# The second mixer of a two-layer trunk: batched loads of B, K, keys, values and x, and stores issued by ScalarE

## The chip, the cores and the metric

The kernel runs on one core of a Trainium2 chip, as one program and in one launch. The metric is the device time of one execution in microseconds; the median of several executions is given. Five engines work side by side: PE (matmuls, with a separate row PEld for its weight loads), DVE and ACT (elementwise work and copies out of PSUM), POOL (small elementwise work and memsets) and SP, which here issues most of the DMAs. Each engine takes its instructions in a fixed order and waits on semaphores for the others.

## The reference

Two layers run over 1040 prompt tokens (16 learned ones ahead) and 64 tokens of a second group. Layer 0 mixes with a gated delta rule, layer 1 with RWKV-7; each is followed by a gated feed-forward part. The change touches the RWKV-7 mixer alone; in short form:

```python
xr, xw, xk, xv, xa, xg = h[None] + xx[None] * mu[:, None, None, :]
r, k, v = (xr @ w_r), (xk @ w_k), (xv @ w_v)
w_log = -softplus(-(w0 + tanh(xw @ w1) @ w2)) - 0.5
a = sigmoid(a0 + (xa @ a1) @ a2)
gate = sigmoid(xg @ g1) @ g2
kk = l2_normalize((k * k_k).reshape(B, T, RWKV_HEADS, RWKV_N))
k = k * (1.0 + (a - 1.0) * k_a)
decay = exp(-exp(w_log))
def step(S, inp):                      # per token, per head, S is 64 x 64
    d_t, kk_t, b_t, v_t, k_t, r_t = inp
    sa = einsum('bhij,bhj->bhi', S, -kk_t)
    S = S * d_t + sa[..., :, None] * b_t + v_t[..., :, None] * k_t
    return S, einsum('bhij,bhj->bhi', S, r_t)
y = group_norm(y) * ln_w + ln_b + sum(r * k * r_k) * v
x = x + (y * gate) @ w_o
```

## The kernel before

Everything is float32; a projection is done as three matmuls on a high and a low part of each operand (lines 130 to 132), with 1024 channels as eight tiles `f` of 128 and 1104 tokens as three groups `g`. The recurrence is computed by chunks of 64 tokens.

The mixer (`rwkv_a`, then `rwkv_b`) has these stages, and keeps what passes between them in DRAM tensors `dr[...]`, most of them eight tiles of 128 x 1152:

- Projection of r and the lora projections w, a and g. `store` writes r, the decay term SW and A (lines 1252 and 1265). The hidden part of the gate goes to HG.
- Key projection, `post_k`: per tile it loads A and SW, and stores PQ, KR[0], BK[0] and BK[1] (lines 1421 to 1428).
- Value projection, `post_v`: per tile it loads PQ, BK[1] and R (1455 to 1457), and stores KR[1], V and the bonus BV (1459 to 1467). The gram matrices of batch 0 and the first half batch are worked on beside it.
- The recurrence, six batches (three groups, four channel tiles each). In batch i, `weave` interleaves `chain` (the recurrence itself, two halves of three chunks), `build` for the half batches of batch i+1, `inverse` of batch i+1, `grams` of batch i+2 and `tail` of batch i-1 (norm, bonus, gate, and the output projection added to x). In batch 0 `gates` stands in the tail's place: it makes the gate from HG and stores it to GT (line 1169).

`build` loads for one channel tile of one half batch: bk by four transfers of 64 x 3 x 64 values (line 1553), kb by two of 64 x 2 x 192 (line 1555) and V by one (1556). The tiles kb live in one of three rooms `z` in turn, one of which lies in the freed space of xT; a room is written again when the chain has ended with the half batch three before. `tail` loads bonus and gate by two transfers (1747, 1749); then for each of eight output tiles it loads x, adds and stores it (1776, 1781, 1783). `inverse` solves 32 x 32 blocks on DVE and POOL, from the tile `dp`, whose last eight blocks are zero since the beginning.

The functions are generators; `weave` sets the order in which the program is written, and a scheduler then orders each engine's instructions by dependence and by its own reckoning, so the order on the engines can be seen only in the built program. Two rules of the program matter: an engine that issues a DMA first waits, in its order, until the data are written and the destination is free; and the DMAs of SP and ACT take one of eight semaphores in turn, and an issue waits until the last DMA on its semaphore has landed.

Of the kernel before, what the change touches and what calls it, by code (L numbers as in the profile page):

```python
# [9 lines left out]
F32 = mybir.dt.float32  # L10
F32R = mybir.dt.float32r
AF = mybir.ActivationFunctionType
ALU = mybir.AluOpType
# [3 lines left out]
P = 128  # L17
# [35 lines left out]
def tile_trunk(ctx, tc, *aps, stages=("gdn", "ffn0", "rwkv", "ffn1"), dbg=None):  # L53
    nc = tc.nc
# [6 lines left out]
    def uid(s):  # L61
        _n[0] += 1
        return f"{s}{_n[0]}"
# [71 lines left out]
    with ExitStack() as es:  # L135
# [6 lines left out]
        ps = psC()  # L142
# [1000 lines left out]
    def gates(tp, xp, dr):  # L1143
        w2 = ins["rwkv_g2"][0]
        hid = []
        for i in range(3):
            t = tp.tile([P, T], F32R, tag=f"hg{i}", bufs=1, name=uid("hg"))
            for c0, n in FULL:
                x = xp.tile([P, 384], F32, tag="ev", name=uid("hx"))
                nc.sync.dma_start(x[:, :n], dr["HG"][i, :, c0:c0 + n])  # L1150
                nc.scalar.copy(t[:, c0:c0 + n], x[:, :n])
            yield
            hid.append(t)
        raws = [rep2(w2[0:128], 1), rep2(w2[128:160], 4)]
        h, l, h2 = (tp.tile([P, KT, P], F32R, tag=f"g2{i}", bufs=1, name=uid("g2")) for i in range(3))
        split(h.rearrange("p a b -> p (a b)"), l.rearrange("p a b -> p (a b)"), raws[0])
        hf = h2.rearrange("p a b -> p (a b)")
        nc.scalar.copy(hf, raws[1])
        nc.vector.tensor_tensor(hf[64:128], raws[1][64:128], hf[64:128].bitcast(F32), ALU.subtract)
        terms = [(h, hid[0]), (h, hid[1]), (l, hid[0]), (h2, hid[2])]  # L1160
        yield
        for f in range(8):
            for g, (c0, n) in enumerate(LIVE):
                ps = psC()
                for i, (w, x) in enumerate(terms):
                    nc.tensor.matmul(ps[:, :n], w[:, f], x[:, c0:c0 + n], start=i == 0, stop=i == 3)
                o = tp.tile([P, 384], F32, tag="go", bufs=2, name=uid("go"))
                nc.scalar.copy(o[:, :n], ps[:, :n])
                nc.sync.dma_start(dr["GT"][f, :, (g + 1) * 384 - n:(g + 1) * 384], o[:, :n])
                yield  # L1170

    def hand_over(tp, xT, c0, n):
# [23 lines left out]
    def rwkv_a(hnp, col, prm, pc, plb, dr, esb, esx, esg, pend, esP):  # L1196
        C = math.exp(-0.5)
        with ExitStack() as es0, ExitStack() as es:
# [43 lines left out]
            def store(ps, n, g, f, name, func=AF.Copy, bias=0.0):  # L1242
                if name == "SW":
                    i = 2 if g else 1
                    e = (sv1 if g else sv0)[cnt[i] % 2]
                    cnt[i] += 1
                    if g == 0:
                        nc.scalar.activation(e[:, 0, 49:65], ps[:, 0:16], func, bias=bias)
                        nc.scalar.activation(e[:, 1:6, 1:65], ps[:, 16:n].rearrange("p (c t) -> p c t", t=64), func, bias=bias)
                    else:  # L1250
                        nc.scalar.activation(e[:, :, 1:65], ps[:, :n].rearrange("p (c t) -> p c t", t=64), func, bias=bias)
                    nc.sync.dma_start(dr["SW"][f, :, 6 * g:6 * g + 6], e)
                else:
                    if g == 0:
                        e = ev0[cnt[0] % 2]
                        cnt[0] += 1
                    else:
                        e = mp.tile([P, 384], F32, tag="ev", name=uid("ev"))
                    if func == AF.Copy and f % 2:
                        nc.vector.tensor_copy(e[:, 384 - n:], ps[:, :n])  # L1260
                    elif func == AF.Copy:
                        nc.scalar.copy(e[:, 384 - n:], ps[:, :n])
                    else:
                        nc.scalar.activation(e[:, 384 - n:], ps[:, :n], func, bias=bias)
                    nc.sync.dma_start(dr[name][f, :, g * 384:(g + 1) * 384], e)

            def dense(s, w, post):
                m = [None] * 3
# [128 lines left out]
            def post_k(ps, n, g, f):  # L1397
# [20 lines left out]
                nc.scalar.activation(c3(pq), l[:, :, 1:65], AF.Exp, scale=-C)  # L1418
                nc.gpsimd.tensor_copy(plb[:, f, 6 * g:6 * g + 6], c3(pq)[:, :, 63])
                cs = slice(g * 384, (g + 1) * 384)  # L1420
                nc.sync.dma_start(dr["PQ"][f, :, cs], pq)
                nc.vector.tensor_tensor(pe, kk, pe, ALU.mult)
                nc.sync.dma_start(dr["KR"][0, f, :, cs], pe)
                bh, kh = tmp("bh"), tmp("kh")
# [20 lines left out]
            with ExitStack() as es, ExitStack() as es1:  # L1445
# [5 lines left out]
                def post_v(ps, n, g, f):  # L1451
# [10 lines left out]
                    nc.tensor.matmul(pn[:, :384], bd1, kh, start=True, stop=True)  # L1462
                    e = ev0[f % 2] if g == 0 else mp.tile([P, 384], F32, tag="ev", name=uid("ev"))
                    nc.scalar.copy(e[:, o:], ps[:, :n])
                    nc.sync.dma_start(dr["V"][f, :, cs], e)
                    nc.vector.tensor_tensor(pq, pn[:, :384], e, ALU.mult)
                    nc.sync.dma_start(dr["BV"][f, :, cs], pq)

                d = dense(3, ins["rwkv_w_v"][0], post_v)
                for _ in range(4):  # L1470
# [24 lines left out]
    class batches:  # L1495
        def __init__(self, dr, tm):
# [5 lines left out]
                    nc.gpsimd.affine_select(mk[r, i], mk[r, i], pattern=[[1, 64]], compare_op=op, fill=0.0,  # L1502
                                            base=0, channel_multiplier=-1)
            self.mkb = mk.unsqueeze(1).to_broadcast([P, 3, 2, 64])
            self.dp = tm.tile([P, 32, 32], F32, tag="rdp", bufs=1, name="rdp")
            nc.gpsimd.memset(self.dp[:, 24:32], 0.0)
            self.pools, self.ttf = [], []

        def home(self, tp):
# [27 lines left out]
        def build(self, i, half):  # L1537
# [2 lines left out]
            tz = self.pools[min(z, 1)]  # L1540
            cs = slice(g * 384 + 192 * half, g * 384 + 192 * half + 192)
            W = B["W"][half] = tz.tile([P, 2, 3, 4, 64], F32, tag=f"W{z}", bufs=1, name=uid("W"))
            for ff in range(4):
                f = 4 * hf + ff
                kb = tz.tile([P, 2, 2, 192], F32, tag=f"kb{z}", bufs=4, name=uid("kb"))
                mb = tz.tile([P, 3, 64], F32, tag=f"mb{z}", bufs=4, name=uid("mb"))
                bt = tz.tile([P, 3, 128], F32, tag=f"bt{z}", bufs=4, name=uid("bt"))
                B["u"][half].append((kb, mb, bt))
                bk = tp.tile([P, 3, 2, 64], F32, tag="bk", bufs=3, name=uid("bk"))
                V = tp.tile([P, 192], F32, tag="V", bufs=2, name=uid("V"))  # L1550
                for q, r in enumerate(HR):
                    for a in range(2):
                        nc.sync.dma_start(bk[r, :, a ^ q], self.dr["BK"][a, f, r, cs].rearrange("p (c t) -> p c t", t=64))
                for q, r in enumerate(HR):
                    nc.sync.dma_start(kb[r, q], self.dr["KR"][:, f, r, cs].rearrange("a p c -> p a c"))
                nc.sync.dma_start(V, self.dr["V"][f, :, cs])
                pt = [psB(), psB()]
                pg = [p[:, :384].rearrange("p (c a t) -> p c a t", a=2, t=64) for p in pt]
                for j in range(3):
# [25 lines left out]
                yield  # L1585

        def inverse(self, i):
            B, tp, dp = self.at(i), self.tm, self.dp
            ttf, at = self.ttf[i % 2], B["at"]
            for b in range(4):  # L1590
                r = slice(32 * b, 32 * b + 32)
# [42 lines left out]
    def rwkv_b(xT, rc, col, plb, dr, Bx, gts, esx, esg, esf, esh, F, more):  # L1634
# [10 lines left out]
        with ExitStack() as esw, ExitStack() as es, ExitStack() as est:  # L1645
# [92 lines left out]
            def tail(g, hf, B):  # L1738
# [4 lines left out]
                cs = slice(g * 384 + o, (g + 1) * 384)  # L1743
                for ff in range(4):
                    f = 4 * hf + ff
                    bv = tp.tile([P, 384], F32, tag="lbv", bufs=lb, name=uid("lbv"))
                    nc.sync.dma_start(bv[:, :n], dr["BV"][f, :, cs])
                    gt = tp.tile([P, 384], F32, tag="lgt", bufs=lb, name=uid("lgt"))
                    nc.sync.dma_start(gt[:, :n], dr["GT"][f, :, cs])
                    pc_ = psC()  # L1750
                    m = 192 - o
                    for a, b, h in ((0, m, 0), (m, n, 1)):
# [8 lines left out]
                    nc.scalar.activation(rs, ps[:, :n], AF.Ln, bias=gne)  # L1761
                    nc.scalar.activation(rs, rs, AF.Exp, scale=-0.5)
                    nc.vector.scalar_tensor_tensor(rs, pc_[:, :n], col("rwkv_ln_w", f), rs, ALU.mult, ALU.mult)
                    nc.vector.scalar_tensor_tensor(rs, rs, col("rwkv_ln_b", f), bv[:, :n], ALU.add, ALU.add)
                    nc.vector.tensor_tensor(rs, rs, gt[:, :n], ALU.mult)
                    split(yy[0][:, ff, :n], yy[1][:, ff, :n], rs)
                    yield
                c0 = LIVE[g][0]
                for mp in range(4):
                    u = wunit(w_o[512 * hf:512 * hf + 512, 256 * mp:256 * mp + 256].rearrange("(k p) c -> p k c", p=P), *wpo)  # L1770
                    wv = [t.rearrange("p (k m) c -> p k m c", m=2) for t in u]
                    for mm in range(2):
                        m = 2 * mp + mm
                        if g < 2:
                            xt = tp.tile([P, 384], F32, tag="xt", bufs=4, name=uid("xt"))[:, :n]
                            nc.sync.dma_start(xt, dr["X"][:, m, c0:c0 + n])
                        else:
                            xt = xT[:, m, c0:c0 + n]
                        ps = psC()
                        mm3(ps[:, :n], (wv[0][:, :, mm], wv[1][:, :, mm]), yy, range(4), n)  # L1780
                        nc.vector.tensor_tensor(xt, xt, ps[:, :n], ALU.add)
                        if g < 2:
                            nc.sync.dma_start(dr["X"][:, m, c0:c0 + n], xt)
                        yield

            def first(tp, hp):
                F.silu = True
# [166 lines left out]
    if dbg and "x" in dbg:  # L1954
        nc.sync.dma_start(dbg["x"], xT)
    if "rwkv" in stages:
        rs_ = {k: dp_.tile([8, P, 1152], F32, name="r" + k) for k in ("V", "GT", "BV", "R")}
        for k in ("KR", "BK"):
            rs_[k] = dp_.tile([2, 8, P, 1152], F32, name="r" + k)
        rs_["X"] = dx  # L1960
        more = "ffn1" in stages
        F, esf, esh = rwkv(xfull, dx, rs_, rc, col, prm, pc, more, pend, esP)
# [46 lines left out]
```

## Time and profile before

| | us |
|---|---|
| median of three timed runs | 3351.06 (3349.12 to 3355.72) |
| the profiled execution's own time | 3353.38 |
| its span, first to last instruction | 3351.6 |
| key projection, value projection (from the trace) | 1770 to 1905, 1905 to 2066 |
| batches 0 to 3 of the recurrence | 2066 to 2160, to 2240, to 2318, to 2398 |

The span is that of one profiled execution; some 2 us lie around it. In the rows below, `xT` also stands for rooms that are cut out of the freed space of the tile xT. A row of waits reads "engine line waited for: total, times, longest"; a row of the chain "start, length, what"; a row of one line's instructions gives the smallest, median and largest duration in ns. SPq and ACTq are the queues of SP and ACT that issue DMAs.

### The profile page before, as it was taken

The page shows a single profiled execution, that of the slowest core. Times are in us where ns is not written, and L with a number is a line of the kernel's source. Part 1 is how long each engine was busy: PE and PEld are TensorE (multiplying, and loading weights), DVE is VectorE, ACT ScalarE, POOL GpSimd, SP SyncE. Part 2 cuts the span into 40 slices and gives each one's busy share as a digit, 9 for nine tenths or more (in the row PEclk, how much of TensorE's full clock was granted, in tenths as well). Part 3 has the DMA queues.
Part 4 walks back from the last instruction along what each step waited for, and adds up shares of the span by engine and source line. Part 5 has one row for each costly group of instructions (what it writes and reads, how often), then busy time and mean ns, then how long its engine had stood idle before and what let it go on. Part 6 is the DMA issues. An engine that isn't in the chain of part 4 may idle for free. (4 is left out here: it accounts for less than half of the span.)

```text
span 3351.6 us, 69660 instructions
## 1 busy us (share of the span) xinstructions
PE 3177.9 (95%) x27426; PEld 2983.6 (89%) x27426; DVE 2505.8 (75%) x5011; ACT 1561.5 (47%) x3134; POOL 293.1 (9%) x539
## 2 busy tenths in 40 slices
PE   7999999898999999999999888888999999999998
PEld 6888888798999999999998777677778999999998
DVE  6967867467777667766879874889986687877775
ACT  5866766434433333213778733434455443333112
POOL 1000000002200000000001130533300310000000
PEclk9999999999999999999999999989999999999999
DMA  5433332884332225422256876445565333335231
GB/s 167 118 99 101 105 91 71 293 278 138 97 98 82 78 75 169 131 83 88 76 184 194 279 227 211 134 141 164 161 192 170 105 97 97 94 94 175 85 98 61
DMA packets 543912, 452.49 MB, mean 135 GB/s; under 512 B 78377, under 2 KB 494930, under 8 KB 543458
## 3 DMA queue, kind: packets, MB, share of 16 engines
q1 hardware_dynamic: 538682, 445.61, 43.2%
q8 instruction: 216, 3.54, 0.4%
q10 hardware_dynamic: 4904, 2.43, 0.3%
q14 instruction: 110, 0.90, 0.1%
HBM read 306.86 MB, written 141.07 MB: 134 GB/s over the span
## 5 line engine op out<-in xcount | busy, mean ns | idle before, releaser
L311 PE MATMUL psA<-tc,sh 128*128 128x276 f32 (+1 forms) x1712 | 500.2, 292 | 20.4 <-DVE hs L319 9.4
L313 PE MATMUL psA<-tc,sl 128*128 128x276 f32 (+1 forms) x1712 | 499.9, 292 | 4.0 <-DVE sl L110 3.9
L312 PE MATMUL psA<-tc,sh 128*128 128x276 f32 (+1 forms) x1712 | 499.4, 292 | 0.3 <-DVE tc L110 0.2
L407 DVE TENSOR_TENSOR xT<-xT,psA 128x384 f32<-128x384 f32 (+3 forms) x496 | 252.4, 521 | 135.0 <-PE psA L132 133.2
L311 PEld LDWEIGHTS psA<-tc,sh 128*128 128x128 f32 x1712 | 327.0, 191 | 22.6 <-DVE hs L319 10.1
L109 ACT CAST wh<-raw 128x1024 fp32r<-128x1024 f32 x159 | 166.3, 1049 | 357.8 <-PE psA L131 239.9
L313 PEld LDWEIGHTS psA<-tc,sl 128*128 128x128 f32 x1712 | 326.5, 191 | 5.0 <-DVE sl L110 4.7
L312 PEld LDWEIGHTS psA<-tc,sh 128*128 128x128 f32 x1712 | 326.6, 191 | 1.2 <-DVE tc L110 0.9
L131 PE MATMUL psA<-hl,wh 128*128 128x384 f32 (+3 forms) x1024 | 326.4, 319 | 0.0
L130 PE MATMUL psA<-hh,wh 128*128 128x384 f32 (+3 forms) x1024 | 325.7, 320 | 0.0
L132 PE MATMUL psA<-hh,wl 128*128 128x384 f32 (+3 forms) x1024 | 325.3, 318 | 0.0
L130 PE MATMUL psA<-hnh,wh 128*128 128x384 f32 (+1 forms) x768 | 269.9, 351 | 5.4 <-ACT hnh L109 4.1
L131 PE MATMUL psA<-hnl,wh 128*128 128x384 f32 (+1 forms) x768 | 262.3, 341 | 1.7 <-DVE hnl L110 1.7
L132 PE MATMUL psA<-hnh,wl 128*128 128x384 f32 (+1 forms) x768 | 261.0, 340 | 0.0
L110 DVE TENSOR_TENSOR wl<-raw,wh 128x1024 fp32r<-128x1024 f32 x159 | 195.0, 1228 | 66.0 <-ACT wh L109 65.5
L109 ACT CAST sh<-raw 128x512 fp32r<-128x512 f32 x202 | 124.9, 621 | 254.9 <-PE psA L312 235.0
L130 PE MATMUL psA<-mxh,wh 128*128 128x384 f32 (+1 forms) x672 | 225.0, 345 | 10.6 <-ACT mxh L109 5.6
L131 PE MATMUL psA<-mxl,wh 128*128 128x384 f32 (+1 forms) x672 | 229.7, 344 | 1.9 <-DVE mxl L110 1.6
L132 PE MATMUL psA<-mxh,wl 128*128 128x384 f32 (+1 forms) x672 | 226.8, 339 | 0.3 <-DVE wl L110 0.3
L130 PEld LDWEIGHTS psA<-hh,wh 128*128 128x128 f32 x1024 | 192.0, 188 | 0.6 <-ACT hh L109 0.4
L132 PEld LDWEIGHTS psA<-hh,wl 128*128 128x128 f32 x1024 | 192.4, 188 | 0.1
L131 PEld LDWEIGHTS psA<-hl,wh 128*128 128x128 f32 x1024 | 192.2, 188 | 0.3
(490 smaller groups left out, 8204.3 us busy)
## 6 DMA issues: line engine op xcount, KB each, us to landing
raw<-in_ffn_w_gate_dram SPq DMA_DIRECT2D x64, 512.0 KB
raw<-in_ffn_w_up_dram SPq DMA_DIRECT2D x64, 512.0 KB
raw<-in_ffn_w_down_dram SPq DMA_DIRECT2D x44, 512.0 KB
raw<-in_gdn_w_in_dram SPq DMA_DIRECT2D x32, 512.0 KB
raw<-in_gdn_w_out_dram SPq DMA_DIRECT2D x24, 512.0 KB
raw<-in_rwkv_w_o_dram SPq DMA_DIRECT2D x24, 512.0 KB
hr<-dhid SPq DMA_DIRECT2D x44, 276.0 KB
hr<-dhid SPq DMA_DIRECT2D x44, 272.0 KB
```

The lines of the kernel that those rows point to most:

```text
L109: nc.scalar.copy(h, src)
L110: (eng or nc.vector).tensor_tensor(l, src, h.bitcast(F32), ALU.subtract)
L130: nc.tensor.matmul(ps, w[0][:, k, :], x[0][:, k, :n], start=a, stop=False)
L131: nc.tensor.matmul(ps, w[0][:, k, :], x[1][:, k, :n], start=False, stop=False)
L132: nc.tensor.matmul(ps, w[1][:, k, :], x[0][:, k, :n], start=False, stop=z)
L311: nc.tensor.matmul(ps, u[0][:, kk], h, start=first and kk == 0, stop=False)
L312: nc.tensor.matmul(ps, u[0][:, kk], l, start=False, stop=False)
L313: nc.tensor.matmul(ps, u[1][:, kk], h, start=False, stop=last and kk == 3)
L407: nc.vector.tensor_tensor(xT[:, m, a:a + n], xT[:, m, a:a + n], pd[:, :n], ALU.add)
```

## The change

- V, PQ, R (even tiles), A, SW and the gate are stored by ACT's queue, which wrote them, instead of SP's.
- BV and GT become one tensor BG, and `tail` loads both parts with one transfer.
- `build` loads kb for all four channel tiles of a half batch at its start, by four transfers of 64 x 4 x 192; bk and V for two channel tiles at a time.
- `tail` loads and stores x by two output tiles, and issues a store only after the first addition of the next pair.
- `dp` is no longer kept: it shares the buffer `b32b` with a later tile of the inverse, and POOL clears its last blocks each time.

```diff
-                nc.sync.dma_start(dr["GT"][f, :, (g + 1) * 384 - n:(g + 1) * 384], o[:, :n])
+                nc.scalar.dma_start(dr["BG"][1, f, :, (g + 1) * 384 - n:(g + 1) * 384], o[:, :n])
...
-                    nc.sync.dma_start(dr["SW"][f, :, 6 * g:6 * g + 6], e)
+                    nc.scalar.dma_start(dr["SW"][f, :, 6 * g:6 * g + 6], e)
...
-                    if func == AF.Copy and f % 2:
+                    q = nc.sync if func == AF.Copy and f % 2 else nc.scalar
+                    if q is nc.sync:
...
-                    nc.sync.dma_start(dr[name][f, :, g * 384:(g + 1) * 384], e)
+                    q.dma_start(dr[name][f, :, g * 384:(g + 1) * 384], e)
...
-                nc.sync.dma_start(dr["PQ"][f, :, cs], pq)
+                nc.scalar.dma_start(dr["PQ"][f, :, cs], pq)
...
-                    nc.sync.dma_start(dr["V"][f, :, cs], e)
+                    nc.scalar.dma_start(dr["V"][f, :, cs], e)
                     nc.vector.tensor_tensor(pq, pn[:, :384], e, ALU.mult)
-                    nc.sync.dma_start(dr["BV"][f, :, cs], pq)
+                    nc.sync.dma_start(dr["BG"][0, f, :, cs], pq)
...
+            f0 = 4 * hf
+            kbs = tz.tile([P, 4, 2, 2, 192], F32, tag=f"kb{z}", bufs=1, name=uid("kb"))
+            for q, r in enumerate(HR):
+                for a in range(2):
+                    nc.sync.dma_start(kbs[r, :, q, a], self.dr["KR"][a, f0:f0 + 4, r, cs].rearrange("f p c -> p f c"))
             for ff in range(4):
-                f = 4 * hf + ff
-                kb = tz.tile([P, 2, 2, 192], F32, tag=f"kb{z}", bufs=4, name=uid("kb"))
+                if ff % 2 == 0:
+                    fs = slice(f0 + ff, f0 + ff + 2)
+                    bks = tp.tile([P, 2, 2, 192], F32, tag="bk", bufs=2, name=uid("bk"))
+                    for q, r in enumerate(HR):
+                        for a in range(2):
+                            nc.sync.dma_start(bks[r, :, a ^ q], self.dr["BK"][a, fs, r, cs].rearrange("f p c -> p f c"))
+                    Vs = tp.tile([P, 2, 192], F32, tag="V", bufs=2, name=uid("V"))
+                    nc.sync.dma_start(Vs, self.dr["V"][fs, :, cs].rearrange("f p c -> p f c"))
+                kb, V = kbs[:, ff], Vs[:, ff % 2]
+                bk = bks[:, ff % 2].rearrange("p a (c t) -> p c a t", t=64)
...
-                bk = tp.tile([P, 3, 2, 64], F32, tag="bk", bufs=3, name=uid("bk"))
-                V = tp.tile([P, 192], F32, tag="V", bufs=2, name=uid("V"))
-                for q, r in enumerate(HR):
-                    for a in range(2):
-                        nc.sync.dma_start(bk[r, :, a ^ q], self.dr["BK"][a, f, r, cs].rearrange("p (c t) -> p c t", t=64))
-                for q, r in enumerate(HR):
-                    nc.sync.dma_start(kb[r, q], self.dr["KR"][:, f, r, cs].rearrange("a p c -> p a c"))
-                nc.sync.dma_start(V, self.dr["V"][f, :, cs])
...
-            B, tp, dp = self.at(i), self.tm, self.dp
+            B, tp = self.at(i), self.tm
+            dp = tp.tile([P, 32, 32], F32, tag="b32b", bufs=1, name=uid("rdp"))
+            nc.gpsimd.memset(dp[:, 24:32], 0.0)
...
-                    bv = tp.tile([P, 384], F32, tag="lbv", bufs=lb, name=uid("lbv"))
-                    nc.sync.dma_start(bv[:, :n], dr["BV"][f, :, cs])
-                    gt = tp.tile([P, 384], F32, tag="lgt", bufs=lb, name=uid("lgt"))
-                    nc.sync.dma_start(gt[:, :n], dr["GT"][f, :, cs])
+                    bg = tp.tile([P, 2, 384], F32, tag="lbg", bufs=lb, name=uid("lbg"))
+                    nc.sync.dma_start(bg[:, :, :n], dr["BG"][:, f, :, cs].rearrange("a p c -> p a c"))
...
+                    if g < 2:
+                        xt = tp.tile([P, 2, 384], F32, tag="xt", bufs=2, name=uid("xt"))[:, :, :n]
+                        nc.sync.dma_start(xt, dr["X"][:, xs, c0:c0 + n])
...
                     for mm in range(2):
...
-                        nc.vector.tensor_tensor(xt, xt, ps[:, :n], ALU.add)
-                        if g < 2:
-                            nc.sync.dma_start(dr["X"][:, m, c0:c0 + n], xt)
+                        nc.vector.tensor_tensor(xt[:, mm], xt[:, mm], ps[:, :n], ALU.add)
+                        if late:
+                            nc.sync.dma_start(*late)
+                            late = None
                         yield
+                    if g < 2:
+                        late = dr["X"][:, xs, c0:c0 + n], xt
+                if late:
+                    yield
+                    nc.sync.dma_start(*late)
```

The scheduler orders the engines anew. On SP, in the middle of the value projection, before (rV, rKR and rBV are stores, pq, kh and rt loads of one tile each, raw a weight):

```order
L1465 DMA rV<-ev_17768 128x384
L1455 DMA pq_22214<-rPQ 128x384
L1467 DMA rBV<-pq_22147 128x384
L1456 DMA kh_22345<-rBK 128x384
L1457 DMA rt_22346<-rR 128x384
L1556 DMA V_22560<-rV 128x192
L117 DMA raw_22586<-in_rwkv_w_v_dram 128x8x128
L1459 DMA rKR<-rt_22216 128x384
L1465 DMA rV<-ev_22225 128x384
L1467 DMA rBV<-pq_22214 128x384
```

and now, at a like place:

```order
L1460 DMA rKR<-rt_21990 128x384
L1458 DMA rt_22061<-rR 128x384
L117 DMA raw_22578<-in_rwkv_w_v_dram 128x8x128
L1456 DMA pq_22059<-rPQ 128x384
L1457 DMA kh_22147<-rBK 128x384
L1468 DMA rBG<-pq_21988 128x384
L1458 DMA rt_22148<-rR 128x384
```

The stores of V are gone from SP; the other two stores of a tile stay among its loads.

On ACT, in the key projection, before (pe, pi and pq are three exponentials of one tile, sq of the next ones):

```order
L1416 ACTIVATE pe_20410<-sw_20395 128x384
L1417 ACTIVATE pi_20411<-sw_20395 128x384
L1418 ACTIVATE pq_20412<-sw_20395 128x384
L1407 ACTIVATE sq_20519<-sq_20519 128x336
L1403 ACTIVATE sq_20575<-psA_20546,prm 128x384
```

and now:

```order
L1417 ACTIVATE pe_20293<-sw_20278 128x384
L1418 ACTIVATE pi_20294<-sw_20278 128x384
L1419 ACTIVATE pq_20295<-sw_20278 128x384
L1404 ACTIVATE sq_20338<-psA_20309,prm 128x384
L1422 DMA rPQ<-pq_20295 128x384
L1404 ACTIVATE sq_20396<-psA_20367,prm 128x384
```

The store of pq stands on ACT, one activation behind the one that writes it. Of the 132 moved stores 98 stand so, with at least one instruction between; 34 follow their write directly.

On SP, in batch 2, where the keys for the second half of batch 3 are loaded (raw is a weight of the output projection), before:

```order
L117 DMA raw_26682<-in_rwkv_w_o_dram 128x4x256
L1776 DMA xt_26688<-dx 128x320
L1553 DMA bk_26709<-rBK 64x3x64 x4
L1555 DMA kb_26706<-rKR 64x2x192 x2
L1556 DMA V_26710<-rV 128x192
L1776 DMA xt_26772<-dx 128x320
L117 DMA raw_26849<-in_rwkv_w_o_dram 128x4x256
L1776 DMA xt_26855<-dx 128x320
L1553 DMA bk_26888<-rBK 64x3x64 x4
L1555 DMA kb_26885<-rKR 64x2x192 x2
```

and now, for the same half batch:

```order
L1553 DMA bk_26549<-rBK 64x2x192 x4
L1555 DMA V_26554<-rV 128x2x192
L1526 DMA b_26838<-rBK 128x384
L1753 DMA lbg_26359<-rBG 128x2x320
L1527 DMA k_26839<-rKR 128x384
L1546 DMA kb_26544<-rKR 64x4x192 x4
L1753 DMA lbg_27225<-rBG 128x2x384
L1553 DMA bk_26891<-rBK 64x2x192 x4
L1555 DMA V_26896<-rV 128x2x192
```

The keys of all four tiles are asked for by four transfers in a row, and what followed the first two of eight now follows all of them.

More of the change, by code (lines that the diff above doesn't have):

```diff
@@ L1504, in __init__ @@
             self.mkb = mk.unsqueeze(1).to_broadcast([P, 3, 2, 64])
-            self.dp = tm.tile([P, 32, 32], F32, tag="rdp", bufs=1, name="rdp")
-            nc.gpsimd.memset(self.dp[:, 24:32], 0.0)
             self.pools, self.ttf = [], []
@@ L1763, in tail @@
                     nc.vector.scalar_tensor_tensor(rs, pc_[:, :n], col("rwkv_ln_w", f), rs, ALU.mult, ALU.mult)
-                    nc.vector.scalar_tensor_tensor(rs, rs, col("rwkv_ln_b", f), bv[:, :n], ALU.add, ALU.add)
-                    nc.vector.tensor_tensor(rs, rs, gt[:, :n], ALU.mult)
+                    nc.vector.scalar_tensor_tensor(rs, rs, col("rwkv_ln_b", f), bg[:, 0, :n], ALU.add, ALU.add)
+                    nc.vector.tensor_tensor(rs, rs, bg[:, 1, :n], ALU.mult)
                     split(yy[0][:, ff, :n], yy[1][:, ff, :n], rs)
@@ L1771, in tail @@
                     wv = [t.rearrange("p (k m) c -> p k m c", m=2) for t in u]
-                    for mm in range(2):
-                        m = 2 * mp + mm
-                        if g < 2:
[L1775 to L1778, printed above, removed]
+                    xs = slice(2 * mp, 2 * mp + 2)
+                    if g < 2:
+                        xt = tp.tile([P, 2, 384], F32, tag="xt", bufs=2, name=uid("xt"))[:, :, :n]
+                        nc.sync.dma_start(xt, dr["X"][:, xs, c0:c0 + n])
+                    else:
+                        xt = xT[:, xs, c0:c0 + n]
+                    for mm in range(2):
                         ps = psC()
                         mm3(ps[:, :n], (wv[0][:, :, mm], wv[1][:, :, mm]), yy, range(4), n)
-                        nc.vector.tensor_tensor(xt, xt, ps[:, :n], ALU.add)
-                        if g < 2:
-                            nc.sync.dma_start(dr["X"][:, m, c0:c0 + n], xt)
+                        nc.vector.tensor_tensor(xt[:, mm], xt[:, mm], ps[:, :n], ALU.add)
+                        if late:
+                            nc.sync.dma_start(*late)
+                            late = None
                         yield
+                    if g < 2:
[3 more added lines that the diff above has]
+                    nc.sync.dma_start(*late)
             def first(tp, hp):
@@ L1956, in tile_trunk @@
     if "rwkv" in stages:
-        rs_ = {k: dp_.tile([8, P, 1152], F32, name="r" + k) for k in ("V", "GT", "BV", "R")}
-        for k in ("KR", "BK"):
+        rs_ = {k: dp_.tile([8, P, 1152], F32, name="r" + k) for k in ("V", "R")}
+        for k in ("KR", "BK", "BG"):
             rs_[k] = dp_.tile([2, 8, P, 1152], F32, name="r" + k)
```

## Prediction

> **What bounds the kernel now.** I read the page first, then a table of stages, then the waits of each stage, then the chain that ended last.
>
> ```profile
> span 3351.6 us, 69660 instructions
> PE 3177.9 (95%) x27426; PEld 2983.6 (89%) x27426; DVE 2505.8 (75%) x5011; ACT 1561.5 (47%) x3134; POOL 293.1 (9%) x539
> ```
>
> PE is busy 95% of the span, so what an edit can give back is in the stages where PE is not busy. The change touches the second mixer alone. The view of stages (start:end, length, then busy time of PE, PEld, DVE, ACT and POOL, granted clock, DMA share, GB/s) shows, in order: the lora projections, the key projection, the value projection, batch 0 with the gates, and batches 2 and 3 of the recurrence. The last line is a short piece of batch 1.
>
> ```profile
> 1657.00:1712.00 55.00, 49.39 (x274) 46.40 (x273) 45.78 (x96) 46.30 (x102) 2.84 (x8) 0.97 0.51 153
> 1770.00:1905.00 135.00, 122.50 (x636) 109.27 (x635) 123.83 (x228) 112.66 (x233) 22.12 (x39) 0.96 0.75 243
> 1905.00:2066.00 161.00, 144.78 (x1141) 124.73 (x1141) 105.01 (x212) 60.41 (x122) 30.31 (x63) 0.95 0.77 238
> 2066.00:2160.00 94.00, 81.78 (x1536) 67.65 (x1535) 70.92 (x168) 41.09 (x97) 31.71 (x71) 0.90 0.47 132
> 2240.00:2318.00 78.00, 69.47 (x1285) 57.93 (x1286) 72.23 (x168) 35.11 (x78) 27.41 (x58) 0.96 0.57 163
> 2318.00:2398.00 80.00, 70.78 (x1259) 58.82 (x1256) 73.41 (x166) 35.42 (x78) 25.53 (x55) 0.94 0.58 166
> 2197.00:2206.00 9.00, 9.00 (x155) 7.14 (x154) 7.84 (x21) 4.27 (x11) 0.00 (x0) 1.00 0.18 48
> ```
>
> PE idles 12.5 us in the key projection, 16.2 in the value projection, 12.2 in batch 0 and 8 to 9 in a later batch, where DVE is busy 72 of 78 us and its work is untouched. Which of this idle time ends with a DMA? Waits of engines, first in the value projection, then (last line) in the key projection; columns are total, times, longest:
>
> ```profile
> PE psC L1462 <- DVE kh L1460: 10.5, 8, 2.3
> DVE rt L1458 <- DMA pq<-rPQ: 13.8, 7, 5.1
> ACT hg L1151 <- DMA hx<-rHG: 14.8, 8, 4.6
> ACT wh L109 <- DMA raw<-in_rwkv_w_v_dram: 4.0, 2, 2.2
> ```
>
> And the waits of the queue that issues, SP: the first line over the whole run, the others from 1950 to 2570 us.
>
> ```profile
> SPq L1421 <- ACT pq L1418: 29.8, 18, 9.1
> SPq L1783 <- DVE xt L1781: 28.6, 12, 7.6
> SPq L1783 <- DVE b32t L601: 12.4, 9, 3.9
> SPq L1465 <- ACT ev L1464: 7.4, 8, 1.5
> SPq L1455 <- DMA rBV<-pq: 4.8, 9, 1.1
> ```
>
> So SP does stand still behind stores, with loads queued behind it. But the place where it stands longest costs nothing:
>
> ```profile
> 2195.15 2.54 SPq L1553 DMA_DIRECT2D bk<-rBK  x4
> 2205.35 0.33 SPq L1783 DMA_DIRECT2D dx<-xt  x1
> 2205.72 1.42 SPq L1555 DMA_DIRECT2D kb<-rKR  x2
> ```
>
> From 2197.7 to 2205.3 SP waits to store x, and a key load waits behind it; in that piece PE is busy 9.00 of 9.00 us (last row of the stages). Removed SP waits therefore count only where a stage shows that somebody was late. The chain that ended last names four loads in the recurrence:
>
> ```profile
> 2078.31 3.25 DMA k<-rKR
> ...
> 2150.75 3.47 DMA xT<-rKR
> ...
> 2311.86 3.13 DMA lgt<-rGT
> ...
> 2364.99 2.45 DMA xT<-rKR
> ```
>
> (xT<-rKR is a key load into the room of xT.)
>
> **The change part by part.** The profiled execution took 3353.4 us, 2.3 over the median of the three timed runs; the terms go against it. What an issue costs:
>
> ```profile
> L1421 SPq DMA_DIRECT2D rPQ<-pq x24: 319/320/571, 1768.5 to 1893.0; - x24
> L1553 SPq DMA_DIRECT2D bk<-rBK x192: 573/605/1717, 1919.2 to 2451.3; - x192
> L1555 SPq DMA_DIRECT2D kb<-rKR x64: 573/607/1596, 2063.4 to 2438.8; - x64
> L1169 SPq DMA_DIRECT2D rGT<-go x24: 319/537/1442, 2060.9 to 2155.4; - x24
> L901 ACTq DMA_DIRECT2D dSZ<-sz x6: 366/370/397, 558.6 to 602.7; - x6
> ```
>
> *Issues that go from SP.* 192 loads of bk become 96 and 96 of kb (64 and 32 into xT) become 48: 96 x 0.605 + 48 x 0.607 = 87 us of SP. 132 stores go to ACT, about 132 x 0.32 = 42 us, more for the gates. SP is not the bound, so I price stage by stage what is late.
>
> *Into the value projection.* ACT waits 4.0 us for two weight loads there. On SP the loads stand behind stores of pq, which wait for ACT. Most of the wait is the transfer itself; I take 1 us saved, from 0 to 4.
>
> *Value projection.* PE waits 10.5 us for kh, which is late because DVE waits 13.8 us for pq loads. The stores of V leave SP (7.4 us of its waits), the wait of a pq load for the landing of the store from the same buffer (4.8) stays, and so does the round trip. I take a third of PE's 10.5, 3.5 us, from 0 to 10.5. The hx loads hold ACT for 14.8 us at the end, while PE still has projections to do; 1 us, from 0 to 5.
>
> *Batch 0.* 24 x 0.537 = 12.9 us of gate stores and about a third of the load issues go from SP; the chain has one 3.25 us load of k, and PE idles 12.2 us of which DVE and ACT end most. 3 us, from 0 to 8.
>
> *Later batches.* The x stores now come one step later (a tail's last one two), and half as many, so SP no longer waits 28.6 + 12.4 us for them; by the piece from 2197 this was covered. One merged load of bonus and gate saves an issue ahead of the 3.13 us lgt load: 1 us, from 0 to 7.
>
> *The key loads get larger.* A half batch now starts with four loads of 192 KB where its first tile needed two of 96 KB. The room comes free only when an earlier half batch has ended, about when the build begins, so they can't be early. Before: 2 x 0.607 plus 2.45 to 3.47 to land, 3.7 to 4.7 us. After: 4 x 0.607 plus the 3.25 us that a 192 KB load of k took, 5.7 us. That is 1 to 2 us more for the first tile, and less for the next three. Two of eleven half batches had such a load in the chain: 2 us lost, from 0 to 11 x 2 = 22. I stay near the low end because only those two show.
>
> *Stores on ACT.* A row of before shows what an issue there costs:
>
> ```profile
> 558.59 0.53 ACT L225 ACTIVATE sg<-sg 128x384 f32<-128x384 f32 x1
> 558.65 0.40 ACTq L901 DMA_DIRECT2D dSZ<-sz  x1
> 559.15 0.53 ACT L226 ACTIVATE sg<-sg 128x384 f32<-128x384 f32 x1
> ```
>
> The queue issues while the engine still computes, and the next activation starts on time. In the built order an activation stands between write and store in most cases, so the cost is near 0; 34 stores (14 of V, 16 of the gates, 4 of R) follow their own write, 34 x 0.37 = 12.6 us, nearly all in stages where ACT is busy 60.41 of 161 and 41.09 of 94 us. If the cover is gone, the key projection pays: ACT 112.66 + 24 x 0.37 = 121.5 of 135. The lora stage, with the 24 stores of SW, would go from 46.30 to 55.2 of 55 if nothing overlapped. I take 1 us lost, from 0 to 13. A new wait comes with it: DMAs share eight semaphores in turn, so an ACT store may wait until an older DMA of SP has landed, and the PSUM copies queue behind it. Three PSUM buffers, each filled by one of 24 tiles in 161 us (about 6.7 us a tile), cover a landing of 3 us.
>
> *The pad of the inverse* moves into a shared buffer and is set in each of six inversions by POOL, which is busy 27.41 of 78 us. The nearest row sets four times as much:
>
> ```profile
> L1598 POOL MEMSET b32t<- x6: 952/952/1099, 1901.7 to 2380.1; 128x1024 f32 x6
> ```
>
> 0, from 0 to 6 x 0.95 = 5.7 lost. The bk matmuls read the same runs of 64 values: 0. The granted clock (0.90 to 0.96 in these stages) I leave as it is.
>
> Sum: -1 -3.5 -1 -3 -1 +2 +1 = -6.5 us, so 3346.9 for the profiled execution; taken from the median 3351.06 it is 3344.6, rounded to **3345**.
>
> **The Trainium skill against it.** The Trainium skill, DMA: Bandwidth & Descriptors, section "Issuing engines are not separate DMA queues", says that transfers begun on several engines run on the same 16 DMA engines, and that only the sequencer's time to begin them is saved. By that rule the moved stores give the 42 us of SP's issue time and nothing else; the piece from 2197 agrees, and it speaks for the second rival. The Trainium skill, Perfetto Trace Analysis, section "DMA Optimizations", says that where DMA engines are mostly idle, splitting a transfer lets some of the work start sooner. The recurrence has a DMA share of 0.47 to 0.58, so that rule speaks against the large key loads, and for the third rival.
>
> **Rivals.**
> 1. *The DMA round trips were the bound of the value projection and batch 0.* For it: the 13.8 and 14.8 us of waits. Against: the round trip remains. It would give all of the upper ends there, 4 + 10.5 + 5, and 2.5 in batch 0, less 2 of loss: -20, 3331.
> 2. *It is hidden anyway.* SP waited, but nobody for SP. For it: PE full during the longest stall, DVE busy 72 of 78 us per batch. Time 3351.
> 3. *The first key tile comes late.* Place: the first tile of a half batch, whose room is freed at a batch's start or in its middle. Each of 11 half batches pays 1 to 2 us, and PE's fixed order puts the recurrence behind it: 11 x 1.5 = +16, less 4 of gains, 3363. It decides from the point where a first tile's matmuls stand within 5.7 us behind the last matmul that read the old keys. Against: PE has the other half's work to do.
>
> **How the numbers follow.** Chances: small gain (3337 to 3351) 0.55, rival 1 0.15, rival 2 0.10, rival 3 0.20. A measurement of this kernel can tell 0.2%, 6.7 us, from no change, so the line is at 3344.4: half of the small gain and rival 1 make 0.42 faster; the other half, rival 2 and a little of rival 3 make 0.39 same; 0.19 slower. The likeliest case alone spans 3337 to 3351. The range for 8 in 10 takes half of rival 1 and most of rival 3: 3328 to 3364.
>
> **What would show it.** Right: the value projection shorter by 3 to 6 us with fewer waits of DVE for pq; batches 2 and 3 within 2 us of 78 and 80; ACT's store rows near 0.37 us with no new idle time behind them. Wrong: key loads in the chain at the start or middle of batches with waits over 5 us (rival 3); ACT idle before its PSUM copies with a DMA named; or the value projection shorter by over 12 us (rival 1). A changed order on PE that moves a stage by several us without a DMA wait would be outside of this reckoning.

## The result, and the profile after

The changed kernel takes 3375.26 us (median of 6 runs), the kernel before 3349.11 in the runs beside it: a ratio of 1.0076, with a 95% interval of 1.0061 to 1.0092. The prediction was 3345 us, and its range ended at 3364. The head of the page of the changed kernel:

```profile
span 3373.9 us, 69301 instructions
...
PE 3179.6 (94%) x27426; PEld 2984.5 (88%) x27426; DVE 2496.9 (74%) x5011; ACT 1563.0 (46%) x3134; POOL 299.9 (9%) x544
```

The engines do the same work, and the span is 22.3 us longer, so time went into waiting or into a slower clock. To find where, I cut both traces at the same instructions and not at the same times. The view of stages of the kernel before, from the first SW sigmoid to the first exponential of the key projection (called the **lora stretch** below), then to the first copy of the value projection, to its last copy, to the start of batch 1's chain, and to the end of batch 5 (columns as above: length, busy time of PE, PEld, DVE, ACT, POOL, granted clock, DMA share, GB/s):

```profile
1664.41:1767.60 103.19, 98.13 (x550) 92.65 (x550) 74.06 (x151) 75.92 (x166) 6.49 (x22) 0.98 0.52 167
1767.60:1913.08 145.48, 132.00 (x684) 118.00 (x685) 133.63 (x247) 119.43 (x247) 22.51 (x40) 0.95 0.76 245
1913.08:2059.41 146.33, 131.97 (x1085) 113.11 (x1083) 94.43 (x189) 52.34 (x105) 30.31 (x63) 0.97 0.77 235
2059.41:2159.69 100.28, 86.20 (x1546) 71.42 (x1546) 73.27 (x176) 43.66 (x103) 31.40 (x71) 0.88 0.49 140
2159.69:2545.18 385.49, 349.99 (x5754) 292.16 (x5754) 329.13 (x739) 173.61 (x377) 103.23 (x211) 0.94 0.54 159
```

The same five stretches of the changed kernel:

```profile
1659.79:1785.46 125.67, 106.51 (x550) 99.22 (x550) 75.06 (x152) 81.90 (x169) 6.82 (x22) 0.91 0.43 138
1785.46:1934.24 148.78, 131.93 (x678) 119.59 (x679) 132.38 (x244) 118.68 (x247) 16.36 (x40) 0.93 0.74 237
1934.24:2087.80 153.56, 134.05 (x1092) 116.28 (x1090) 95.84 (x191) 52.86 (x108) 31.36 (x64) 0.96 0.77 238
2087.80:2180.19 92.39, 80.49 (x1567) 66.19 (x1568) 68.85 (x166) 43.86 (x104) 27.87 (x57) 0.96 0.59 177
2180.19:2566.27 386.08, 347.77 (x5736) 288.12 (x5732) 324.59 (x749) 172.79 (x377) 119.05 (x228) 0.96 0.49 149
```

The lora stretch alone is 22.5 us longer, as much as the whole span. The others add up to +3.2 (+3.3, +7.2, -7.9, +0.6), and the changed kernel comes to the lora stretch 4.6 us earlier. In the lora stretch both kernels run 550 matmuls; PE's idle time (length less busy) goes from 5.1 to 19.2 us, and its busy time from 98.1 to 106.5 as the granted clock falls from 0.98 to 0.91. Whom does PE wait for? One of the three large groups of matmuls in this stretch, before and then after (busy time, mean ns, idle time ahead and who ended it); the other two have under 1 us of idle time ahead of them:

```profile
L130 PE MATMUL psA<-mxh,wh 128*128 128x384 f32 (+1 forms) x152 | 49.8, 338 | 1.6 <-ACT mxh L109 1.5
```

```profile
L130 PE MATMUL psA<-mxh,wh 128*128 128x384 f32 (+1 forms) x152 | 52.0, 362 | 13.7 <-ACT mxh L109 13.7
```

PE waits for the casts that ACT makes of the next mix (mxh). A piece of the changed kernel's timeline shows what stands ahead of such a cast:

```profile
1674.52 0.58 ACT L1251 ACTIVATE sv<-psA,prm 128x384 f32<-128x384 f32 x1 [0.21 <-DMA rSW<-sv]
...
1675.95 0.58 ACT L1251 ACTIVATE sv<-psA,prm 128x384 f32<-128x384 f32 x1 [0.85 <-DMA rSW<-sv]
1676.01 0.88 ACTq L1252 DMA_DIRECT2D rSW<-sv  x2
1676.93 0.51 ACT L109 CAST mxh<-md 128x384 fp32r<-128x384 f32 x1 [0.40 <-ACT sv L1251]
...
1677.49 0.97 PE L130 MATMUL psA<-mxh,wh 128*128 128x384 f32 x2 [4.16 <-ACT mxh L109]
```

Two sigmoids stand ahead of the cast. Each waits until an older store from its buffer has landed, two stores are issued, and the cast starts 0.40 us behind the end of the second sigmoid; PE has had nothing for 4.16 us. And the clock does not come back at once. The two stretches of 3.4 us behind that gap:

```profile
1677.60:1681.00 3.40, 3.40 (x11) 3.02 (x12) 3.40 (x8) 2.83 (x6) 0.00 (x0) 0.50 0.12 42
1681.00:1684.40 3.40, 3.40 (x15) 3.40 (x14) 3.40 (x9) 2.33 (x5) 0.00 (x0) 0.61 0.00 0
```

The granted clock is 0.50, then 0.61. The Trainium skill, TensorE: Matmul & The Clock Gate, section "What's actually happening", has a rule for this: a PE that has been idle for a window of about 3.4 us is given half its pulses until it has been busy for such a window. The trace agrees with its 0.50; the last section shows shorter gaps that do the same. The changed kernel has three gaps of 3.5 to 4.2 us in this stretch, each followed by 3.4 us at 0.50. The kernel before has none over 1.9 us inside it. (Each of the two has one more that ends in the first 0.4 us of the stretch: 3.55 us before, 2.82 us after.)

Two things can have made the loss, and they are told apart below. **Theory I**: issuing from ACT takes ACT's time, 0.33 us and a wait for the write just ahead. **Theory O**: the scheduler, which plans each engine's order, made another order for the changed program, and that order is worse, whoever issues. The built programs do differ: with only the R, SW and A stores moved, from the first R copy to the first key exponential 143 of 271 computing instructions of ACT, 163 of 278 of DVE and 336 of 908 of PE stand at another place.

### The profile page after: what moved, and what is told of

Read it like the earlier page. It is cut to its first block, busy times and chain, and to the rows that moved or that the text cites. A ratio compares the mean times of both kernels' runs of the same rounds, so it can differ in the third digit from the quotient of the medians.

```text
span 3373.9 us, 69301 instructions
## 1 busy us (share of the span) xinstructions
PE 3179.6 (94%) x27426; PEld 2984.5 (88%) x27426; DVE 2496.9 (74%) x5011; ACT 1563.0 (46%) x3134; POOL 299.9 (9%) x544
```

## The experiments

All times in one table. Medians of 4 to 12 runs, the ratio to the kernel before in runs beside them with its 95% interval, and from the profiled run the lengths of the five stretches. "Key" and "value" are the two projections.

| run | median us | ratio | lora | key | value | batch 0 | batches 1-5 |
|---|---|---|---|---|---|---|---|
| before | 3349.11 | | 103.2 | 145.5 | 146.3 | 100.3 | 385.5 |
| after | 3375.26 | 1.0076 (1.0061 to 1.0092) | 125.7 | 148.8 | 153.6 | 92.4 | 386.1 |
| e1 | 3348.38 | 0.9994 (0.9978 to 1.0009) | 105.0 | 146.9 | 150.5 | 95.1 | 387.2 |
| e2 | 3362.80 | 1.0037 (1.0020 to 1.0055) | 123.1 | 149.1 | 150.5 | 94.8 | 375.9 |
| e3 | 3363.61 | 1.0044 (1.0028 to 1.0061) | 104.8 | 159.0 | 153.8 | 92.3 | 388.3 |
| e4 | 3368.29 | 1.0057 (1.0038 to 1.0076) | 123.2 | 150.4 | 145.4 | 100.3 | 388.0 |
| e5 | 3355.82 | 1.0029 (1.0013 to 1.0045) | 113.7 | 145.2 | 149.8 | 98.7 | 386.6 |
| e6 | 3371.28 | 1.0069 (1.0047 to 1.0091) | 121.9 | 145.4 | 147.4 | 100.2 | 385.0 |
| e7 | 3349.82 | 1.0003 (0.9989 to 1.0016) | 104.7 | 143.8 | 152.9 | 96.0 | 384.5 |
| e8 | 3357.31 | 1.0024 (1.0008 to 1.0039) | 104.0 | 159.2 | 144.5 | 93.9 | 387.1 |
| e9 | 3362.32 | 1.0038 (1.0023 to 1.0052) | 112.9 | 146.8 | 152.0 | 95.9 | 384.4 |
| e10 | 3343.97 | 0.9982 (0.9970 to 0.9994) | 102.5 | 146.4 | 145.6 | 91.9 | 389.7 |
| e11 | 3401.72 | 1.0153 (1.0136 to 1.0170) | 121.8 | 161.3 | 161.8 | 109.8 | 390.4 |
| e12 | 3347.30 | 1.0000 (0.9987 to 1.0013) | 104.3 | 149.3 | 148.2 | 92.1 | 387.1 |
| e13 | 3371.89 | 1.0064 (1.0043 to 1.0085) | 125.7 | 146.3 | 147.1 | 100.9 | 387.6 |
| e14 | 3350.39 | 1.0008 (0.9994 to 1.0023) | 103.8 | 144.8 | 149.4 | 95.3 | 387.4 |
| e15 | 3348.94 | 0.9989 (0.9976 to 1.0003) | 103.5 | 148.1 | 146.8 | 101.1 | 383.3 |

A single stretch of one run is not exact to a few us: in the runs with no store of V on ACT (e11 left out) the value projection lies between 144.5 (clock 0.99) and 152.9 (clock 0.92). The profiled execution can also lie some us off the median (e5: 3363.09). The lora stretch is either 102.5 to 105.0 or 112.9 and more, so there it decides.

### The stores or the loads: e1 to e4

**e1**, the changed kernel with all its stores on SP:

```diff
-                    nc.scalar.dma_start(dr["SW"][f, :, 6 * g:6 * g + 6], e)
+                    nc.sync.dma_start(dr["SW"][f, :, 6 * g:6 * g + 6], e)
-                    q.dma_start(dr[name][f, :, g * 384:(g + 1) * 384], e)
+                    nc.sync.dma_start(dr[name][f, :, g * 384:(g + 1) * 384], e)
... and so for PQ, V and the gate rows
```

> The changed kernel with all five kinds of store that it gave to ScalarE back on SyncE; batched loads, late x stores and the merged bonus/gate load stay. Theory S (issuing stores from ScalarE delays the mix and the lora stage, batching itself gains some 6 to 10 us in the recurrence, as the chain starts show): 3341 to 3352 us, the first K exponential within 3 us of the kernel before. Theory B (the batched loads or late stores cost the time): 3370 us or more.

**e2**, the kernel before with these stores on ACT and nothing else:

> The kernel before with only the five kinds of store moved to ScalarE; loads, x stores and gate rows as before. Theory S: 3370 to 3385 us, the lora stage some 20 us longer than before. Theory B: 3345 to 3355 us.

**e3**, as e1, but with PQ, V and the gate rows still on ACT:

> The changed kernel with only the R, SW and A stores back on SyncE; the PQ, V and gate stores stay on ScalarE. Theory S, with its cost in the lora stage: 3350 to 3358 us, the value projection still some 8 us longer. Theory B: 3370 us or more. If the loss belongs to PQ and V stores and only shows early: about 3365 us.

**e4**, the kernel before with the R, SW and A stores on ACT (the first two lines of the diff, the other way):

> The kernel before with only the R, SW and A stores moved to ScalarE. Theory S: 3366 to 3374 us, all of it by the first K exponential. Theory B: 3345 to 3355 us.

e1 gives the loss back (3348), e4 makes most of it alone (+19 us, lora 123.2), e2 makes the lora stretch as long (123.1). So it is the move of the stores (theory S), and the batched loads are neither gain nor loss beyond the measurement; the 6 to 10 us that theory S expected of them in the recurrence do not show. e2 in all came out below what was expected, 3362.80, with batches 1 to 5 at 375.9 us. e3 was a miss for theory S: the lora stretch is short again, but the time is 3363.61, near the 3365 of the third case, and the key projection takes 159.0 us, which the changed kernel does not show (148.8). A cost that comes and goes with an edit in another stretch speaks for an order, not for the issuing.

### Issuing or order: e5 and e6

Here the issuing engine and the order are set apart. The program of e4 and that of before hold the same computing instructions, so the order that one has can be laid on the other, as constraints on the order of issue alone, which add no wait:

```diff
         tile_trunk(tc, *args)
+        at = {i.name: i for i in nc.cur_bb.bb.instructions}
+        for o in ORDER:                 # one list for each of ACT, DVE and PE
+            for a, b in zip(o, o[1:]):
+                tc.add_manual_dep(at[f"I-{b}"], f"I-{a}", _mybir.DependencyInfo(
+                    _mybir.DependencyClass.NoSync, _mybir.DependencyReason.DATA), reason="order")
```

**e5** is e4 with before's order from the first R copy to the first key exponential; **e6** is before (all stores on SP) with e4's order there.

> The kernel before with the R, SW and A stores issued by ScalarE, but with the computing instructions of ScalarE, VectorE and TensorE, from the first R copy to the first K exponential, held to the very order that they have in the kernel before (the stores lie among them where the scheduler puts them). Theory I (the issuing itself and its wait for the write just ahead hold ScalarE up): 3363 to 3372 us, from the first SW sigmoid to the first K exponential about 120 us. Theory O (the scheduler's other order does it): 3347 to 3355 us, and 103 to 107 us for that stretch.

> The kernel before with all its stores on SyncE, but with the computing instructions of ScalarE, VectorE and TensorE from the first R copy to the first K exponential held to the order that they take when ScalarE issues the R, SW and A stores. Theory I: 3345 to 3353 us, and 103 to 107 us from the first SW sigmoid to the first K exponential. Theory O: 3362 to 3372 us, and 118 to 123 us. Both theories half: about 112 us in either of this pair of runs.

The lora stretch of e5, then of e6, then the wait of PE in e6:

```profile
1661.65:1775.38 113.73, 104.36 (x550) 95.96 (x550) 74.88 (x151) 78.75 (x167) 6.55 (x22) 0.95 0.47 152
```

```profile
1662.96:1784.81 121.85, 106.11 (x550) 99.47 (x550) 74.90 (x151) 80.29 (x168) 6.83 (x22) 0.90 0.44 141
```

```profile
PE psA L130 <- ACT mxh L109: 10.8, 4, 3.8
```

e6 issues nothing from ACT in this stretch and still loses all of it: 3371.28 us, 121.9 in the stretch, the same wait of PE for mxh, a clock of 0.90. That the other order alone makes the loss is shown. But theory I is not nothing: the time of e5 is 0.8 us above the range of theory O, and its stretch lies midway between the two. With the old order, issuing from ACT costs 10.5 us of the stretch (113.7) and 7 us in all. The two do not add: in the new order issuing costs 1.4 us more of the stretch (e4 123.2 against e6 121.9) and nothing that can be measured in all (1.0057 against 1.0069).

### The same on the changed kernel, and the gates: e7 to e9, e11, e12

**e7** leaves only the gate rows on ACT, **e8** only PQ (as e1, but for that line):

> The changed kernel with only the gate rows' stores left on ScalarE, the other four kinds back on SyncE. Theory I (a store costs where ScalarE has work queued that others wait for; at the gates it has little): 3342 to 3348 us, batch 0 some 2 us shorter than with all stores on SyncE. Rival (any store on ScalarE costs): 3350 to 3356 us.

> The changed kernel with only the PQ stores left on ScalarE, the other four kinds back on SyncE. If the PQ stores are what makes the key projection 12 us longer in the kernel with R, SW and A on SyncE: 3357 to 3363 us, the key projection near 159 us. If that length came from the V or gate stores, or from the two together: 3346 to 3353 us and near 147 us.

**e12** is e8 with the order of e1 on ACT, DVE and PE through the key and value projections (its list ends there; from batch 0 on the order is its own); **e9** is the changed kernel with before's order up to the first copy of the value projection; **e11** is the kernel before with the changed kernel's order throughout:

> The changed kernel with only the PQ stores on ScalarE, and the computing instructions of ScalarE, VectorE and TensorE held throughout to the order that they have with all stores on SyncE. If the 12 us of the key projection are the scheduler's order: 3346 to 3353 us and 147 to 150 us for the key projection. If they are the issuing: 3356 to 3363 us and 156 us or more.

> The changed kernel, all its stores and loads as they are, with the computing instructions of ScalarE, VectorE and TensorE up to the first copy of the value projection held to their order in the kernel before. Theory O (most of the loss is the scheduler's other order, the rest the issuing): 3353 to 3363 us, the stretch from the first SW sigmoid to the first K exponential about 114 us instead of 126. Theory I: 3370 us or more.

> The kernel before, all stores on SyncE and no load batched, with the computing instructions of ScalarE, VectorE and TensorE held to their order in the changed kernel throughout. Theory O: 3363 to 3375 us, 118 us or more from the first SW sigmoid to the first K exponential. Theory I: 3345 to 3353 us.

The key projection of e8, then of e12:

```profile
1765.32:1924.50 159.18, 134.50 (x685) 119.47 (x686) 132.23 (x244) 121.48 (x247) 21.89 (x40) 0.92 0.71 224
```

```profile
1762.35:1911.66 149.31, 133.05 (x684) 119.36 (x685) 132.91 (x246) 119.67 (x247) 21.83 (x40) 0.94 0.74 239
```

PQ's 10 us of e8 go when the order is held (3347.30 us): order again. Its ratio of 1.0000 also shows that holding an order through these stages costs nothing that can be measured. e7 met neither expectation: 3349.82 lies between them, and batch 0 is no shorter than in e1 (96.0 against 95.1), so the gate stores neither cost nor gain anything that can be measured. e9 takes 13 of the 26 us back from the changed kernel, with its stores and loads untouched, and its lora stretch of 112.9 equals that of e5, as theory O and a remainder from issuing say. So on the changed kernel the old order gives back 12.8 of the 22.5 us of this stretch, and 9.7 stay with the stores on ACT. e11 was a miss on the far side: 3401.72. An order that was planned for ACT's stores and batched loads is worse still on a kernel that has neither; beside the lora stretch the key projection, the value projection and batch 0 lose 15.8, 15.4 and 9.5 us against before.

### What the issuing itself costs: e13

In e5, 17 of the 60 stores stand directly behind the write that they store, and 38 have one computing instruction between. e13 puts all 60 directly behind, with the order of before still held:

> As the run with ScalarE's R, SW and A stores in the order of before, but each of the 60 stores put directly behind the write that it stores (17 stood there, 38 had one instruction between). If the wait for that write's end holds ScalarE up: 43 more such waits at some 0.3 us lengthen the stretch from the first SW sigmoid to the first K exponential by 4 to 13 us over its 114, and the time is 3359 to 3368 us. If only the issue time of 0.33 us or the completion of older stores counts: 111 to 116 us, and 3353 to 3359 us.

```profile
1661.26:1786.95 125.69, 106.73 (x548) 95.97 (x546) 74.45 (x150) 80.21 (x167) 6.47 (x22) 0.95 0.42 137
```

One row of the changed kernel's SW stores, durations in ns:

```profile
L1252 ACTq DMA_DIRECT2D rSW<-sv x24: 326/326/368, 1659.8 to 1711.1; - x24
```

An issue takes 0.326 us, near the 0.370 of the row that the prediction used. The issues in e13 are as many as in e5, and the stretch grows by 12.0 us over e5, 0.28 us for each of the 43 stores that moved up to their write. In the same stretch the waits of ACT that its own last write ended grow from 2.4 us (6 times) to 12.5 (30 times), and those of PE for mxh from 5.2 to 13.9. So a store directly behind its write costs ACT the wait for that write; the total (3371.89) lies a little above the expected 3368. How the 10.5 us of e5 itself divide is not shown: only 2.4 us are such waits.

### What is left of the gains: e10, e14, e15

**e10** is e1 with keys and values loaded by single tiles again; **e14** and **e15** are the kernel before with only the late two-tile x stores, and with only the merged bonus and gate load:

```diff
-                        nc.sync.dma_start(bks[r, :, a ^ q], self.dr["BK"][a, fs, r, cs].rearrange("f p c -> p f c"))
+                        nc.sync.dma_start(bks[r, ff % 2, a ^ q], self.dr["BK"][a, f, r, cs])
... and so for kb and V
```

> The changed kernel with all stores on SyncE and the keys and values of the recurrence loaded one tile at a time again; the merged bonus and gate load and the late x stores stay. If batch 0 is some 5 us shorter because of the batched key loads: 100 us for batch 0 again, and the value projection back to 146 us. If the merged load or the queue without x stores shortens it: 95 us. The total in either case 3344 to 3353 us.

> The kernel before with only the x loads and stores made two tiles wide and the store put one matmul group later. If this part made the run with loads by tile faster: 3343 to 3346 us. If it is hidden (SyncE's queue does not bound batches 1 to 3): 3347 to 3351 us.

> The kernel before with only the bonus and gate rows in one tensor and read by one transfer. If this part shortens batch 0 (100 us in the kernel before, 92 in the run with loads by tile): 92 to 96 us there and 3342 to 3346 us in all. If it is hidden: 99 to 101 us and 3347 to 3351 us.

e10 is the one version whose interval lies below the kernel before, by 0.06 to 0.30%. Its batch 0 is 8 us shorter than before, below both lengths that were expected, and batches 1 to 5 are 4 us longer. The x stores (1.0008) do not give that alone. The merged load (0.9989, batch 0 at 101.1) does not shorten batch 0, but its interval overlaps that of e10, so a part of the gain can be its own. Batch 0 is 5 us shorter in e14, where nothing that batch 0 stores or loads was changed. So a small gain is measured, but which part makes it is open; the order, which differs in each of these programs, was not held equal here.

## Why the prediction was wrong, step by step

- **Stores on ACT: +1, from 0 to 13. The step that failed.** R, SW and A alone measured +19 (e4). The reckoning held that "an activation stands between write and store in most cases, so the cost is near 0", from a row of another stage (line 901) where ACT's next activation had nothing to wait for. The count of 34 direct stores also let another store stand for the instruction between: without that, the built program of the changed kernel has 46, and 11 of the 12 more are SW and A stores of the lora stretch. Where ACT was busy 46.30 of 55 us and PE waited on it, issuing the 60 stores cost 10.5 us of the lora stretch (e5), within the bound of 13. What no bound held was the order: it was taken as fixed but for the moved rows, while 336 of 908 PE rows moved. The last sentence of the text put that outside of the reckoning; it was 18.7 us by itself (e6), and both together 20.0 (e4). Why the scheduler chose this order stays open.
- **"The granted clock I leave as it is": failed with it.** Of the 22.5 us in the lora stretch 8.4 are PE's longer busy time at the lower clock, and each of the three new gaps is followed by 3.4 us at 0.50.
- **Value projection: -3.5, from 0 to -10.5.** Not found. The round trips stay, and so do the waits; the three rows of the changed kernel that answer to those shown of before:

```profile
DVE rt L1459 <- DMA pq<-rPQ: 14.8, 10, 4.1
...
ACT hg L1151 <- DMA hx<-rHG: 12.2, 7, 4.6
...
PE psC L1463 <- DVE kh L1461: 11.2, 8, 2.3
```

 The wait for kh is 11.2 us (10.5 before) and that for pq loads 14.8 (13.8). Taking stores off SP did not shorten these waits. The wait for hx is 2.6 us less, but PE had waited only 0.6 us for what ACT makes of hx (L1166, before). The stretch is 7.2 us longer; e1, e7 and e10 (150.5, 152.9, 145.6), where V is stored by SP, spread as widely, so the cause of that part is not settled.
- **Into the value projection: -1.** ACT's wait for w_v in the key projection fell from 4.0 to 1.2 us, but the key projection became 3.3 us longer.
- **Batch 0: -3, from 0 to -8.** -7.9 in the trace, -5.2 in e1. The sign was right; that DMA issues did it is not shown (e14, e15).
- **Later batches and larger key loads: -1 and +2.** Together +0.6 over batches 1 to 5, near the forecast; but this stretch lies anywhere between 375.9 and 390.4 us in the table, so the agreement shows little. The key loads went no slower to issue (573/608/1449 ns; 573/607/1596 before), and none stands in the chain any more at the start or middle of batches 1 to 5:

```profile
L1546 SPq DMA_DIRECT2D kb<-rKR x32: 573/608/1449, 2091.6 to 2444.1; - x32
```

- **Rivals.** The first (round trips as the bound) forecast a gain of 20 us, and the kh row shows none of it. That round trips bound the stage is not refuted by this: the chain that ended last of the changed kernel runs through some in the value projection (the landing of a store, then the load into the same buffer), where that of before has none until 2036 us:

```profile
1935.47 5.35 DMA rBG<-pq
1940.83 2.74 DMA pq<-rPQ
```

 But the chain of e10, with one of the shortest value projections (145.6), has them too. The third, with which the slow side was reached, did not happen: the time came out slow by another mechanism. The second (hidden anyway) is what the loads and x stores did: e1 0.9994, e14 1.0008, e15 0.9989.

## What to carry to other kernels

Where a scheduler sets the order, a change of the engine that issues a DMA can change every engine's order: compare the built orders of the engines that wait for each other, and when a stage moves, lay the old order on the new program before blaming the edit. Move stores to a compute engine only where nobody waits for its next instruction, and keep at least one computing instruction between the write and its store. Price a gap of PE at more than its length: in the lora stretch 14.1 us of added gaps brought 8.4 us of slower matmuls, an estimate of 0.6 us for each us of gap.

## What the runs showed of the hardware that was not expected

Gaps below 3.4 us can halve the clock too, but not each of them does. In e6 PE waits 2.38 us, and runs at 0.50 and then 0.59 after it:

```profile
1678.36 0.97 PE L130 MATMUL psA<-mxh,wh 128*128 128x384 f32 x2 [2.38 <-ACT mxh L109]
```

```profile
1678.25:1681.65 3.40, 3.29 (x10) 2.92 (x11) 3.32 (x7) 2.83 (x7) 0.00 (x0) 0.50 0.67 204
1681.65:1685.05 3.40, 3.40 (x14) 3.40 (x14) 3.40 (x9) 2.33 (x5) 0.00 (x0) 0.59 0.00 0
```

Later in the same run PE waits 2.38 us once more (2027.35 to 2029.72), and the 3.4 us behind that gap run at 1.00; in e10 even a gap of 3.00 us (to 1829.33) is followed by 1.00. From the first R copy to the last copy of the value projection, the traces of all 17 kernels have 44 gaps of PE over 3.0 us, and each is followed by 3.4 us at a granted clock of 0.50 to 0.66. Of the 51 gaps of 2.2 to 3.0 us, 43 are followed by 0.50 to 0.80 and 8 by 1.00; behind the 53 of 1.8 to 2.2 us it is anything from 0.50 to 1.00. So between 1.8 and 3.0 us the length alone does not decide; what does stays open.
